# adaLN products in steps of 256 columns by half the features, the halves summed when evicted

## The chip, the cores and the metric

One NeuronCore of a Trainium2 chip runs the whole program. The metric is the device time of one execution in microseconds. The engines are named as in the profile: PE (matrix products; PEld are its weight loads), DVE, ACT and POOL (element-wise work), SP (issues DMAs). ACT and POOL issue DMAs too, each in its own queue of instructions.

## What is computed

Two layers of a hybrid backbone over 512 latent and 256 context tokens of 1024 features. Each layer starts with shift, scale and gate vectors from a conditioning vector, one for the latents (`c`) and one for the context (`c_ctx`):

```python
def layer_forward(x, xc, cos, sin, c, c_ctx, w_ada, b_ada, ...):
    shift, scale, gate = jnp.split(jax.nn.silu(c) @ w_ada + b_ada, 3, axis=-1)
    shift_c, scale_c, gate_c = jnp.split(jax.nn.silu(c_ctx) @ w_ada + b_ada, 3, axis=-1)
    h = rms_norm(x) * (1.0 + scale[:, None]) + shift[:, None]
...
    p = h @ w_in
...
    x = x + gate[:, None] * (jnp.concatenate([ya, yb, yc], axis=-1) @ w_out)
```

`w_ada` is 1024 x 3072 in float32 for each layer: 24 blocks of 128 columns, 8 each for shift, scale and gate. Between `p` and the last line stand three branches: a chunked MLP with gelu (`ya`), a bidirectional state-space scan, SSD (`yb`), and differential attention with four heads, rotary embedding and two score maps per head whose softmaxes are subtracted (`yc`). The second layer ends with a norm and updates only the latents.

## The kernel before

The program is written once for a layer and run for both. A scheduler places the instructions of all engines in one pass over a timeline of its own; the code gives it priorities (`HPada` and the like lift the DMAs of a block), `PACE` ties single projections to marks in the attention, so that the attention stays ahead of them, and buffers in rings (three of 512 KB, tag `raw`, for all weights that come from memory; two PSUM banks, tag `acc`, for projections and adaLN products). Each engine then runs its own list in order: an instruction that waits holds back all that follow it on that engine.

A layer runs in three stages. First the norm, the input projection of the SSD's blocks and the scan. Then the attention, from about 365 us in layer 0 and 1115 us in layer 1. Beside it PE works through the projections of the other branches: tiles `accz`, `accuv`, `accu`, `accga`, each a block of 128 columns in parts `hi` and `lo`. `scores` makes one score map (`sm`, L749 and L752), DVE its row maximum (`mx`, L754), ACT its exponentials (`Ea`, L756); `weights` transposes their difference (`ptw`, L777), `values` multiplies by v (`pO`, L790), normalises (`osq`, L791 and L798), transposes back (L799) and multiplies by the gate (`gg`, L801). `roped` loads a head's q or k block and its turned copy (`qrq`, `qrk`, `qsq`, `qsk`, L685 and L687) in SP's queue and rotates it on DVE (L689 to L691). Last the output projection: four groups of features (`kq` 4, 8, 0, 12 in layer 1), two halves of 512 columns, `oacc` L1025 to L1027. Its weights come as `wo` and are split into `wohi` on ACT and `wolo` on DVE (L145, L146). The mixed features are written to memory as `ydr` by `finish` (`yhi` and `ylo`, L434 in ACT's queue, L435 in POOL's) and are read back as `yl` (L1020, ACT's queue).

The shift, scale and gate of layer 0 that aren't needed at once are computed beside the attention by `ada_steps`: 24 steps in layer 0 (8 for its gate, 16 for layer 1's shift and scale) and 8 in layer 1 (its gate). A step is one block of 128 columns: SP loads it (`wa`, L194, 128 partitions x 8 x 128 float32), eight matmuls (L198) with 32 columns of weights each, `sc`, which are zero but for the two conditioning vectors, go to the four column groups of the array in turn, features 0 to 511 starting a sum in PSUM and features 512 to 1023 ending it, and ACT copies the bank to a quarter of `part` (L199). After four steps `ada_second` sums the four column groups with a matmul by `sel`.

Of the kernel before, what the change touches and what calls it, by code (L numbers as in the profile page):

```python
# [11 lines left out]
F32 = mybir.dt.float32  # L12
# [79 lines left out]
def tile_hybrid_trunk(ctx: ExitStack, tc: tile.TileContext, ins, out: bass.AP):  # L92
# [93 lines left out]
    def ada_steps(mp, todo):  # L186
        """todo: (layer, its index, first of four blocks); one step for each block"""
        pend = None
        for L, li, b0 in todo:
            part = mp.tile([P, 4, P], F32, tag="part", bufs=NPART, name=f"part{li}_{b0}")  # L190
            for i in range(4):
                with tc.high_priority(HPada):
                    wa = wpool.tile([P, KD, P], F32, tag="raw", bufs=NRAW, name=f"wa{li}_{b0}_{i}")
                    nc.sync.dma_start(wa, ins["w_ada"][li, :, P * (b0 + i) : P * (b0 + i) + P].rearrange("(k p) m -> p k m", p=P))  # L194
                pa = bank("acc", f"pa{li}_{b0}_{i}")
                for k in range(KD):
                    j = k % 4
                    pe.matmul(pa[32 * j : 32 * j + 32, :P], sc[:, k, :], wa[:, k, :], start=k < 4, stop=k >= 4)  # L198
                act.activation(part[:, i, :], pa[:, :P], AF.Copy)  # L199
                if pend:  # L200
                    ada_second(mp, *pend)
                    pend = None
                yield
            pend = L, li, b0, part
        ada_second(mp, *pend)
# [45 lines left out]
    def first_layer_in(L, sp, sx, ws, w_split):  # L251
        """norm and modulation of the inputs by feature blocks, the first projections beside it"""
# [6 lines left out]
        def ada_in(k):  # L259
            """shift and scale of feature block k"""  # L260
            with tc.high_priority((HPW0, HPW1, HPW)[min(k, 2)] if FL else HPW):
                wa = [sp.tile([P, KD, P], F32, tag="Fb", bufs=4, name=f"wa0_{k}_{i}") for i in range(2)]
                for i in range(2):
                    c0 = DM * i + P * k
                    nc.sync.dma_start(wa[i], ins["w_ada"][0, :, c0 : c0 + P].rearrange("(k p) m -> p k m", p=P))
            pa = bank("sc", f"pa0_{k}")
            for i in range(2):
                for q in range(KD):
                    j = q % 4
                    pe.matmul(pa[32 * j : 32 * j + 32, P * i : P * i + P], sc[:, q, :], wa[i][:, q, :], start=q < 4, stop=q >= 4)  # L270
            part = small.tile([P, 2, P], F32, tag="part0", name=f"part0_{k}")
            act.activation(part, pa[:, 0:256].rearrange("p (i m) -> p i m", i=2), AF.Copy)
            for i in range(2):
                pe.matmul(pa[:, 256 + 2 * i : 258 + 2 * i], part[:, i, :], sel, start=True, stop=True)
                dve.tensor_scalar(
                    L.mod[:, 8 * i + k, :], pa[:, 256 + 2 * i : 258 + 2 * i], L.b_ada[:, 8 * i + k : 8 * i + k + 1], float(i), ALU.add, ALU.add
                )
# [65 lines left out]
    for li in range(DEPTH):  # L343
# [67 lines left out]
        def silu_block(c0, name):  # L411
            """2 * silu of a projected block"""
# [16 lines left out]
        def finish(kt, y, t3=t3):  # L429
            """a finished block of the mixed features, in two parts"""  # L430
            hi = t3(f"yhi{li}_{kt}", dt=F32R)
            lo = t3(f"ylo{li}_{kt}", dt=F32R)
            split(hi[:, tl0:], lo[:, tl0:], y[:, tl0:])
            Q["yh"].dma_start(ydr[0, kt, :, tl0:], hi[:, tl0:].bitcast(F32))  # L434
            Q["yl"].dma_start(ydr[1, kt, :, tl0:], lo[:, tl0:].bitcast(F32))  # L435

        # ================= SSD =================
        with tc.tile_pool(name=f"ssd{li}", bufs=1, reuse_waits="tile") as sp, tc.tile_pool(name=f"ssx{li}", bufs=1, reuse_waits="tile") as sx, tc.tile_pool(name=f"ps_s{li}", bufs=3, space=PSUM, reuse_waits="tile") as ps2:
# [32 lines left out]
            def seg_proj(w, s, tag, name):  # L471
                """three passes of one block's product over one segment"""
# [82 lines left out]
            for g in range(2):  # L555
# [24 lines left out]
                def state(t, d, H_in):  # L580
                    """state after chunk t in direction d"""
# [76 lines left out]
            # projections that are kept for the attention  # L658
# [7 lines left out]
        # ================= attention; beside it the other branches' gates =================  # L666
        with ExitStack() as zstack, ExitStack() as mstack, ExitStack() as astack:
# [13 lines left out]
            def roped(idx, lonly, name):  # L681
                """a head's projected block, both parts of it, latents rotated"""
# [49 lines left out]
            def scores(H, h, t):  # L732
                """exponentials of one query tile's two (negated, scaled) score maps, their sums"""
# [27 lines left out]
            def weights(H, h, t, Es):  # L761
                """difference of the two maps, transposed"""
# [111 lines left out]
            def gelu2_block(c0, name):  # L874
                """2 * gelu of a projected block"""
# [98 lines left out]
        with tc.tile_pool(name=f"outa{li}", bufs=1, reuse_waits="tile") as oa, tc.tile_pool(name=f"outb{li}", bufs=1, reuse_waits="tile") as op, tc.tile_pool(name=f"ps_o{li}", bufs=NOA, space=PSUM, reuse_waits="tile") as ps2:  # L974
# [8 lines left out]
            # ================= output projection, gated residual =================  # L983
# [5 lines left out]
            for n in range(2):  # L989
# [20 lines left out]
                def product(t, qs):  # L1010
                    """part of one token tile's product"""
# [116 lines left out]
```

## Time and profile before

| | |
|---|---|
| median of three runs | 1448.0 us (1446.86 to 1449.85) |
| the profiled execution, its span | 1448.3 us |
| PE busy | 1337.9 us, 92% |
| DVE busy | 945.3 us, 65% |
| ACT busy | 656.1 us, 45% |
| POOL busy | 214.5 us, 15% |
| the chain that ended last | PE 53%, DMA 18%, issue 12%, DVE 9%, ACT 6% |
| `pa` matmul records beside the attention | 512, in 32 steps |

All durations below are from that one execution. A row of the timeline is the start, the duration, the engine with its line, the operation, output <- inputs, and how many like it follow one another; in brackets the idle time before it and what ended it. ACTq and SPq are those engines' DMA issues.

### The profile page before, as it was taken

Reading aid. Unit: us, or ns where it says so; the run is one execution under the profiler, and the core shown is the slowest. Engines: PE = TensorE matmul, PEld = TensorE weight load, DVE = VectorE, ACT = ScalarE, POOL = GpSimd, SP = SyncE. Lnnn points to the kernel's source line nnn. Section 1 sums busy time; section 2 is a strip of 40 time slices with the busy share of each in tenths; the row PEclk is TensorE's granted clock in tenths of the full one; section 3 lists DMA queues with packets and bytes.
Section 4 is the critical chain, followed back from the end, with each engine's and each line's share of the span. In section 5 each row is a group of like instructions: output and inputs, shape, how many; then the busy total and the mean of one; then the engine's idle time right before and its main releaser. Section 6 shows DMA issues by size and latency. Waiting matters only on the chain.

```text
span 1448.3 us, 21208 instructions
## 1 busy us (share of the span) xinstructions
PE 1337.9 (92%) x7944; PEld 1101.8 (76%) x7944; DVE 945.3 (65%) x1465; ACT 656.1 (45%) x1406; POOL 214.5 (15%) x418
## 2 busy tenths in 40 slices
PE   4999999999988999999999989999999689989987
PEld 3787888778867787788887768778778557778765
DVE  4497897587576657775232458887677477787432
ACT  3257634624455547554121235833623455575320
POOL 2002023113101113220000000202213001222000
PEclk8999999999999989999999999999999899989999
DMA  9424255745937447567878522625737954557885
GB/s 290 125 74 131 72 164 169 204 127 189 310 112 200 138 138 237 168 202 255 249 236 238 160 67 64 161 84 164 219 102 205 255 155 127 188 161 231 267 270 162
DMA packets 271782, 255.97 MB, mean 177 GB/s; under 512 B 14384, under 2 KB 223552, under 8 KB 271680
## 3 DMA queue, kind: packets, MB, share of 16 engines
q1 hardware_dynamic: 176624, 126.07, 31.1%
q0 software_dynamic: 18800, 66.68, 14.7%
q10 hardware_dynamic: 76256, 61.88, 13.9%
q8 instruction: 62, 1.02, 0.3%
q14 instruction: 40, 0.33, 0.1%
HBM read 199.12 MB, written 49.17 MB: 171 GB/s over the span
## 4 chain that ended last, share of the span: by engine, by line
PE 53%; DMA 18%; issue 12%; DVE 9%; ACT 6%; POOL 2%; SPq 1%; ACTq 0%; DVEq 0%; POOLq 0%
PE oacc L1027 4%; PE oacc L1026 4%; PE oacc L1025 4%; DMA Fb<-csd 3%; DMA yl<-ydr 3%; DMA qsq<-kq 2%; PE pS L585 2%; PE accc L387 2%; PE accc L391 2%; PE accc L392 2%; ACT Fb L608 2%; PE pO L790 2%; DMA qsk<-kq 2%; PE po L640 2%; PE acck L387 2%
## 5 line engine op out<-in xcount | busy, mean ns | idle before, releaser
L608 ACT ACTIVATE Fb<-Fb,dt_fp 128x128 f32<-128x128 f32 x320 | 98.6, 392 | 89.2 <-DVE Fb L605 89.2
L387 PE MATMUL accc<-h_hi,whic 128*128 128x512 f32 (+1 forms) x312 | 108.5, 348 | 5.5 <-ACT xp L451 3.8
L391 PE MATMUL accc<-h_lo,whic 128*128 128x512 f32 (+1 forms) x312 | 107.2, 344 | 0.0
L392 PE MATMUL accc<-h_hi,wloc 128*128 128x512 f32 (+1 forms) x312 | 106.8, 342 | 0.3 <-DVE wloc L146 0.3
L1025 PE MATMUL oacc<-wohi,yl 128*128 128x512 f32 x240 | 95.1, 396 | 5.0 <-DMA yl<-ydr 3.9
L1027 PE MATMUL oacc<-wohi,yl 128*128 128x512 f32 x240 | 95.4, 397 | 2.8 <-DMA yl<-ydr 2.8
L456 DVE SCALAR_TENSOR_TENSOR yv<-xp,hal,yv 128x772 f32<-128x772 f32 (+1 forms) x96 | 94.1, 993 | 5.7 <-ACT yv L454 4.5
L1026 PE MATMUL oacc<-wolo,yl 128*128 128x512 f32 x240 | 94.8, 395 | 1.0 <-DVE wolo L146 1.0
L756 ACT ACTIVATE Ea<-sm,mx 128x768 f32<-128x768 f32 (+1 forms) x80 | 65.2, 816 | 47.9 <-DVE mx L754 34.7
L605 DVE TENSOR_TENSOR Fb<-Fb,dt_cs 128x1024 f32<-128x1024 f32 x40 | 48.8, 1221 | 50.1 <-DMA Fb<-csd 50.0
L754 DVE TENSOR_REDUCE mx<-sm 128x1 f32<-128x768 f32 (+1 forms) x80 | 67.1, 843 | 13.6 <-PE sm L752 13.5
L387 PE MATMUL accz<-h_hi,whiz 128*128 128x512 f32 (+1 forms) x192 | 71.9, 375 | 0.8 <-DVE gtz L426 0.4
L391 PE MATMUL accz<-h_lo,whiz 128*128 128x512 f32 (+1 forms) x192 | 70.3, 366 | 0.0
L392 PE MATMUL accz<-h_hi,wloz 128*128 128x512 f32 (+1 forms) x192 | 70.1, 365 | 0.0
L387 PEld LDWEIGHTS accc<-h_hi,whic 128*128 128x128 f32 x312 | 59.4, 190 | 13.9 <-ACT xp L451 5.1
L749 PE MATMUL sm<-kh,qq 128*128 128x256 f32 (+1 forms) x144 | 52.5, 382 | 14.6 <-ACT Ea L756 12.9
L790 PE MATMUL pO<-v,wt 128*128 128x128 f32 x416 | 59.4, 295 | 6.5 <-DVE gg L801 4.8
L637 POOL DMA_DIRECT2D EF<-ecd x72 | 44.7, 627 | 139.3 <-DVE xT L642 128.3
L392 PEld LDWEIGHTS accc<-h_hi,wloc 128*128 128x128 f32 x312 | 59.5, 191 | 7.3 <-DVE wloc L146 0.5
L391 PEld LDWEIGHTS accc<-h_lo,whic 128*128 128x128 f32 x312 | 59.4, 190 | 6.8 <-issue 0.7
L790 PEld LDWEIGHTS pO<-v,wt 128*128 128x128 f32 x416 | 55.2, 207 | 11.6 <-DVE gg L801 5.5
L1043 DVE TENSOR_TENSOR go<-oacc,gate 128x512 f32<-128x512 f32 x20 | 13.7, 687 | 70.9 <-PE oacc L1027 70.9
(374 smaller groups left out, 3874.5 us busy)
## 6 DMA issues: line engine op xcount, KB each, us to landing
yl<-ydr ACTq DMA_DIRECT2D x120, 256.0 KB
wa<-in_w_ada SPq DMA_DIRECT2D x48, 512.0 KB
Fb<-csd POOLq DMA_DIRECT2D x40, 512.0 KB, 5.9
wo<-in_w_out SPq DMA_DIRECT2D x32, 512.0 KB
rawc<-in_w_in SPq DMA_DIRECT2D x22, 512.0 KB
EF<-ecd POOLq DMA_DIRECT2D x72, 128.0 KB, 3.1
rawz<-in_w_in SPq DMA_DIRECT2D x16, 512.0 KB
ydr<-yhi ACTq DMA_DIRECT2D x12, 384.0 KB
```

The lines of the kernel that those rows point to most:

```text
L387: m = pe.matmul(acc[:, :n], hi[:, k, :], h_hi[:, k, o : o + n], start=k == 0, stop=False)
L391: pe.matmul(acc[:, :n], hi[:, k, :], h_lo[:, k, o : o + n], start=False, stop=False)
L392: pe.matmul(acc[:, :n], lo[:, k, :], h_hi[:, k, o : o + n], start=False, stop=k == KD - 1)
L456: dve.scalar_tensor_tensor(yv[:, lo_:], xp[:, lo_ + tap : tap + W2], L.convh[:, j, tap : tap + 1], yv[:, lo_:], ALU.mult, ALU.add)
L608: act.activation(Fb[:, h, :], Fb[:, h, :], AF.Exp, bias=fp[:, o : o + 1])
L749: m = pe.matmul(c_, H.qs[i][:, tsl], H.kh[i][:, k0 : k0 + kn], start=True, stop=False)
L754: dve.tensor_reduce(mx[:, i : i + 1], smap[:, s0 : s0 + nk], AX.X, ALU.min)
L756: act.activation(Es[i], smap[:, s0 : s0 + nk], AF.Exp, bias=mx[:, i : i + 1], scale=-1.0, accum_out=z[:, i, t % 2 : t % 2 + 1])
L790: pe.matmul(o_, H.w[:, k, P * ql : P * ql + P], H.v[:, k, :], start=k == 0, stop=k == nkt - 1)
L1025: pe.matmul(accs[t], yh[0][:, k, :], whi, start=q == 0 and k == 0, stop=False)
L1026: pe.matmul(accs[t], yh[0][:, k, :], wlo, start=False, stop=False)
L1027: pe.matmul(accs[t], yh[1][:, k, :], whi, start=False, stop=q == 3 and k == 3)
```

## The change

Every step now takes 256 columns and half of the features. Four matmuls of 256 columns go to the four column groups, each starting and ending its sum. The first half's bank is copied by ACT to two quarters of `part`; the second half's bank is added to them by DVE. A step's load has the same 512 KB in rows of 1 KB instead of 512 bytes. The number of steps, the order of blocks, the buffers and the priorities are the same. The lines of the changed kernel behind this place are five higher. The rest of the diff takes comments and docstrings away.

```diff
-            for i in range(4):
-                with tc.high_priority(HPada):
-                    wa = wpool.tile([P, KD, P], F32, tag="raw", bufs=NRAW, name=f"wa{li}_{b0}_{i}")
-                    nc.sync.dma_start(wa, ins["w_ada"][li, :, P * (b0 + i) : P * (b0 + i) + P].rearrange("(k p) m -> p k m", p=P))
-                pa = bank("acc", f"pa{li}_{b0}_{i}")
-                for k in range(KD):
-                    j = k % 4
-                    pe.matmul(pa[32 * j : 32 * j + 32, :P], sc[:, k, :], wa[:, k, :], start=k < 4, stop=k >= 4)
-                act.activation(part[:, i, :], pa[:, :P], AF.Copy)
-                if pend:
-                    ada_second(mp, *pend)
-                    pend = None
-                yield
+            for c in range(2):
+                for half in range(2):
+                    r0, c0 = 4 * P * half, P * b0 + 256 * c
+                    with tc.high_priority(HPada):
+                        wa = wpool.tile([P, 4, 256], F32, tag="raw", bufs=NRAW, name=f"wa{li}_{b0}_{c}_{half}")
+                        nc.sync.dma_start(wa, ins["w_ada"][li, r0 : r0 + 4 * P, c0 : c0 + 256].rearrange("(k p) m -> p k m", p=P))
+                    pa = bank("acc", f"pa{li}_{b0}_{c}_{half}")
+                    for j in range(4):
+                        pe.matmul(pa[32 * j : 32 * j + 32, :256], sc[:, 4 * half + j, :], wa[:, j, :], start=True, stop=True)
+                    dst, pv = part[:, 2 * c : 2 * c + 2, :], pa[:, :256].rearrange("p (i m) -> p i m", m=P)
+                    if half == 0:
+                        act.activation(dst, pv, AF.Copy)
+                    else:
+                        dve.tensor_tensor(dst, dst, pv, ALU.add)
+                    if pend:
+                        ada_second(mp, *pend)
+                        pend = None
+                    yield
```

The scheduler runs anew, and from the first of these steps on the lists of all engines differ. Three places follow; in a name the first digit is the layer, the last number a running one.

DVE at the start of layer 0's attention, before: the rope products of head 1's q and k, then the first two reductions of score maps.

```order
L689 TENSOR_TENSOR qsk0_1_3571<-qsk0_1_3571,sin0_3405 128x512
L690 TENSOR_TENSOR qrq0_1_3588<-qrq0_1_3588,cos0_3404 128x512
L691 TENSOR_TENSOR qrk0_1_3569<-qrk0_1_3569,qsk0_1_3571 128x512
L754 TENSOR_REDUCE mx0_0_0_3458<-sm0_0_0_1_3459 128x1
L754 TENSOR_REDUCE mx0_0_0_3458<-sm0_0_0_0_3465 128x1
```

The same place after:

```order
L694 TENSOR_TENSOR qsk0_1_3571<-qsk0_1_3571,sin0_3405 128x512
L695 TENSOR_TENSOR qrq0_1_3588<-qrq0_1_3588,cos0_3404 128x512
L204 TENSOR_TENSOR part0_16_4689<-part0_16_4689,pa0_16_1_1_4946 128x256
L696 TENSOR_TENSOR qrk0_1_3569<-qrk0_1_3569,qsk0_1_3571 128x512
L759 TENSOR_REDUCE mx0_0_0_3458<-sm0_0_0_1_3459 128x1
L759 TENSOR_REDUCE mx0_0_0_3458<-sm0_0_0_0_3465 128x1
```

The addition of the second half has come between the rope products, ahead of the first reduction.

PE at the end of layer 1's attention, before: the last of the two transpositions of `pO1_3_2`, the last attention work, within the output product `oacc1_0`.

```order
L1025 MATMUL oacc1_0_3_12323<-wohi1_0_0_12256,yres1_0_12067 128x512
L799 MATMUL pO1_3_2_11071<-ident_75,osq1_3_2_11073 128x128
L1026 MATMUL oacc1_0_3_12323<-wolo1_0_0_12257,yres1_0_12067 128x512
L1027 MATMUL oacc1_0_3_12323<-wohi1_0_0_12256,yres1_1_12068 128x512
L1025 MATMUL oacc1_0_4_12368<-wohi1_0_2_12232,yl1_0_4_4_0_12369 128x512
```

After:

```order
L1032 MATMUL oacc1_0_5_12285<-wohi1_0_0_12128,yres1_1_11940 128x512
L804 MATMUL pO1_3_2_10975<-ident_75,osq1_3_2_10977 128x128 x2
L1030 MATMUL oacc1_0_2_12150<-wohi1_0_1_12134,yres1_0_11939 128x512
L1030 MATMUL oacc1_0_3_12195<-wohi1_0_1_12134,yres1_0_11939 128x512
L1030 MATMUL oacc1_0_4_12240<-wohi1_0_1_12134,yres1_0_11939 128x512
```

The last transposition stands 62 matmuls of the output product later, and the rows behind them are those that read `wohi1_0_1`.

ACT at the same place, before: from the last block's `yhi` to the loads of the last group of features.

```order
L145 ACTIVATE yhi1_15_11097<-gg1_3_10766 128x512
L434 DMA ydr1_7714<-yhi1_15_11097 128x512
L1020 DMA yl1_0_5_8_0_12430<-ydr1_7714 128x4x128
L1020 DMA yl1_0_5_8_1_12432<-ydr1_7714 128x4x128
L145 ACTIVATE wohi1_0_1_12262<-wo1_0_1_12260 128x1024
L145 ACTIVATE wohi1_0_6_12268<-wo1_0_6_12266 128x1024
L145 ACTIVATE wohi1_0_7_12274<-wo1_0_7_12272 128x1024
L1020 DMA yl1_0_2_12_0_12458<-ydr1_7714 128x4x128
```

After:

```order
L145 ACTIVATE yhi1_15_11001<-gg1_3_10670 128x512
L439 DMA ydr1_7618<-yhi1_15_11001 128x512
L1025 DMA yl1_0_2_12_0_12330<-ydr1_7618 128x4x128
L1025 DMA yl1_0_3_12_0_12353<-ydr1_7618 128x4x128
L1025 DMA yl1_0_4_12_0_12376<-ydr1_7618 128x4x128
L145 ACTIVATE wohi1_0_1_12134<-wo1_0_1_12132 128x1024
L145 ACTIVATE wohi1_0_6_12140<-wo1_0_6_12138 128x1024
L145 ACTIVATE wohi1_0_7_12146<-wo1_0_7_12144 128x1024
```

Three loads that read the `ydr` rows just written have moved ahead of the conversion `wohi1_0_1`. Further on, `yl1_0_5_12`, the last loads of the first half, stood behind the conversion of `wohi1_1_1` on ACT; now its two parts stand behind those of `wohi1_1_4` and `wohi1_1_5`, three and two conversions of second-half weights earlier.

## Rows read from the trace of the kernel before

**Rows 1.** The page, busy time of each engine, share of the span, instructions.

```profile
PE 1337.9 (92%) x7944; PEld 1101.8 (76%) x7944; DVE 945.3 (65%) x1465; ACT 656.1 (45%) x1406; POOL 214.5 (15%) x418
```

**Rows 2.** Windows: stretch, length, busy us of PE, PEld, DVE, ACT, POOL; clock; DMA share; GB/s.

```profile
365.00:400.00 35.00, 33.28 (x241) 27.90 (x238) 18.01 (x32) 15.62 (x31) 3.28 (x6) 1.00 1.03 312
1115.00:1357.00 242.00, 212.00 (x1179) 170.37 (x1178) 166.59 (x272) 128.26 (x269) 41.83 (x73) 0.94 0.66 194
1260.00:1280.00 20.00, 13.96 (x69) 10.29 (x67) 19.60 (x32) 15.71 (x35) 6.91 (x13) 0.80 0.74 226
```

**Rows 3.** The tile `pa`: count, ns min/median/max, first and last start, forms.

```profile
L198 PEld LDWEIGHTS pa<-wa,sc x512: 106/109/173, 373.1 to 1205.6; 128*32 128x32 f32 x171
L198 PE MATMUL pa<-wa,sc x512: 272/273/419, 373.1 to 1205.7; 128*32 128x128 f32 x171
...
L199 ACT ACTIVATE part<-pa x32: 259/277/300, 374.4 to 1206.9; 128x128 f32<-128x128 f32 x32
...
L272 ACT ACTIVATE part<-pa x8: 383/383/384, 22.1 to 59.9; 128x256 f32<-128x256 f32 x8
```

**Rows 4.** Timeline of PE: the first step of the products.

```profile
373.06 0.64 PE L198 MATMUL pa<-wa,sc 128*32 128x128 f32 x16
```

**Rows 5.** Timeline of DVE: an operation on two tiles of 128x256.

```profile
405.52 0.43 DVE L888 TENSOR_TENSOR gquv<-gquv,geuv 128x256 f32<-128x256 f32 x1
```

**Rows 6.** The page, DMA queues: packets, MB, share of 16 engines' span.

```profile
q1 hardware_dynamic: 176624, 126.07, 31.1%
q0 software_dynamic: 18800, 66.68, 14.7%
```

**Rows 7.** Timeline of SP's issues, start of layer 0's attention.

```profile
395.13 0.40 SPq L194 DMA_DIRECT2D wa<-in_w_ada  x1
402.03 0.53 SPq L687 DMA_DIRECT2D qsk<-kq  x1
```

**Rows 8.** Timeline of PE, DVE and ACT, end of layer 1's attention.

```profile
1356.73 0.27 PE L799 MATMUL pO<-ident,osq 128*128 128x128 f32 x1
...
1357.04 0.48 DVE L801 SCALAR_TENSOR_TENSOR gg<-gg,hal,pO 128x256 f32<-128x256 f32 x1 [7.77 <-PE pO L799]
...
1357.56 0.63 ACT L145 ACTIVATE yhi<-gg 128x512 fp32r<-128x512 f32 x1 [5.97 <-DVE gg L801]
1358.22 0.34 ACTq L434 DMA_DIRECT2D ydr<-yhi  x1
1360.02 0.98 ACTq L1020 DMA_DIRECT2D yl<-ydr  x2
1361.04 1.06 ACT L145 ACTIVATE wohi<-wo 128x1024 fp32r<-128x1024 f32 x1 [2.85 <-PE oacc L1027]
...
1362.74 0.37 ACTq L1020 DMA_DIRECT2D yl<-ydr  x1
```

**Rows 9.** The tile `ydr`, its stores from issue to landing.

```profile
DMA to landing us min/median/max: 2.3/3.8/7.8
```

**Rows 10.** Timeline of ACT and PE, the output product's change of halves in layer 1.

```profile
1375.54 1.06 ACT L145 ACTIVATE wohi<-wo 128x1024 fp32r<-128x1024 f32 x1 [1.60 <-DMA wo<-in_w_out]
...
1381.43 1.06 ACT L145 ACTIVATE wohi<-wo 128x1024 fp32r<-128x1024 f32 x1 [1.52 <-DMA wo<-in_w_out]
1381.51 0.94 ACTq L1020 DMA_DIRECT2D yl<-ydr  x2
...
1388.19 0.80 PE L1025 MATMUL oacc<-wohi,yl 128*128 128x512 f32 x1 [3.50 <-DMA yl<-ydr]
...
1390.42 0.80 PE L1027 MATMUL oacc<-wohi,yl 128*128 128x512 f32 x1 [1.00 <-DMA yl<-ydr]
```

**Rows 11.** The chain that ended last, same stretch: start, us, what.

```profile
1381.94 8.44 DMA yl<-ydr
...
1394.20 0.43 PE oacc L1026
...
1395.04 0.23 PE oacc L1025
```

## The prediction

> **What bounds the kernel now.** I read the page's busy times first. PE is busy 1337.9 of 1448.3 us [rows 1], so a change earns only where PE stands idle, or where its clock is down. The windows come next: they show where that is. In the first 35 us of layer 0's attention the DMA engines are full (share 1.03) while PE is busy 33.28 of 35; over layer 1's attention, 1115 to 1357 us, PE is busy 212.00 of 242, so 30 us are idle, and 20 us of it, 1260 to 1280, have PE 13.96 busy at clock 0.80 with DVE 19.60 busy [rows 2]. The tile view of `pa` gives the price of a step's parts [rows 3], the timeline one whole step [rows 4]. Last I followed the end of layer 1 in the timeline, since the order lists differ there most [rows 8 to 10].
>
> **The products.** A step before is eight fp32 matmuls, sixteen records, four at a time on the four column groups: 0.64 us from first start to last end [rows 4]. A step after is four matmuls, eight records, of twice the columns. If four still run at once, that is half as many rounds of twice the length, and nothing changes. If they ran one after another, eight records of two times 0.109 us (the median weight load, which paces them [rows 3]) make 1.74 us instead of 0.64: 32 x 1.10 = +35 us. Not needing to add up in PSUM could at best take the last round's tail away, 0.27 x 32 / 2 = -4 us. I take **0**, since the sixteen records in 0.64 us show the groups at work side by side and nothing in the change ties them together. All of it would lie on the path, PE being the bound.
>
> **The evictions.** ACT loses 32 x 0.277 = 8.9 us and gets 16 x 0.383 (a 128x256 eviction at the kernel's start) = 6.1 us [rows 3]. ACT is busy 45% [rows 1]: 2.7 us less there is worth nothing by itself. DVE gets 16 additions of 128x256; the nearest row is a 128x256 sum of two tiles, 0.43 us [rows 5], so 6.9 us on an engine that is 65% busy. An addition waits for its matmuls, and what is queued behind it on DVE waits too. At one place that is on the path: at the start of layer 0's attention the addition of `pa0_16_1_1` now stands between two rope products and ahead of `mx0_0_0`, the reduction for which the first exponentials wait. There it costs its 0.43 us, **+0.4**. Elsewhere the additions stand beside projections, and PE covers them; if all sixteen were on the path it would be +6.9.
>
> **The transfers.** Bytes and number of DMAs stay; packets go from 1024 of 512 bytes to 512 of 1 KB. Two queues give a price: q1 moved 126.07 MB in 176624 packets in 31.1% of 16 engines' span, which is 40.8 ns per packet of 714 bytes; q0 66.68 MB in 18800 packets in 14.7%, 181 ns per 3547 bytes [rows 6]. A line through both gives 30.8 ns for 512 bytes, 56.2 for 1 KB (an estimate): a step's transfer falls from 1.97 to 1.80 us of all sixteen engines, by 0.17. Only where the engines are full and an awaited load lies behind in SP's queue does it count. In the two attention starts seven `wa` issues stand ahead of an awaited `qsq` or `qsk` (one pair shown, `wa` at 395.13 and `qsk` at 402.03 [rows 7]): 7 x 0.17 = **-1.2**. The ends are 0 (the transfers hidden) and 32 x 0.17 = -5.4. The Trainium skill, "DMA: Bandwidth & Descriptors", section Specifications, puts the smallest transfer at line rate at 512 bytes; by that the packets before were as good as those after, the term would be 0 and the sum 1.2 us more. The two queues' prices don't settle it, since they hold other sizes too.
>
> **The order.** The scheduler places everything again, and from the first steps on the lists differ. Two places matter.
>
> *1260 to 1280 us.* Here PE has no projections, only score maps, and waits for DVE. After, a like run exists, earlier in the heads: six score maps again, with 30 DVE rows from the first reduction to the last instead of 35. With 19.60 us for 32 rows in the window [rows 2] five fewer are 3.0 us; half of the clock's loss, 20 x 0.20 x 13.96/20 / 2 = 1.4, goes with it: **-4.4**. Ends: 0 if DVE's rest is only moved, and 6.0 + 2.8 = -8.8 if all goes.
>
> *The end of layer 1's attention.* Before, the last transposition of `pO1_3_2` ends at 1357.0 and PE has 134 matmuls of the output product's first half left [rows 8], at 0.23 us each at full clock [rows 11]. After, both transpositions stand behind 120 of its 192 matmuls, and the next PE row needs `wohi1_0_1`. On ACT that conversion stood behind `yl1_0_5_8`; now it stands behind `yhi1_15`, its store to `ydr` and three loads of `yl` that read the store. So PE waits for a chain: from the transposition's end 0.04 to `gg`, 0.48, 0.04, `yhi` 0.63, 0.03, so the store's issue 1.2 us later [rows 8]; landing 2.3 us, the shortest of the `ydr` stores [rows 9] (the first load that reads this one went out at 1362.74, which bounds it at 4.5 [rows 8]); three loads at 0.49; the conversion 1.06 [rows 8]. 1.2 + 2.3 + 1.5 + 1.06 = **+6.0**, and 8.2 by the long landing. After waits of 3.50 and 1.00 us [rows 10] some twelve matmuls went 0.43 us apart instead of 0.23 [rows 11], at the lower of the clock's two levels: **+2.4** for a second such wait.
>
> Then the old wait. Before, PE waits 4.5 us for `yl1_0_5_12`, issued at 1381.51 behind the conversions of the second half's weights, which follow `wohi1_0_1` by 14.5 (`wohi1_1_5`) and 20.4 us (`wohi1_1_1`) [rows 8, 10]. After, the later of the two loads stands behind `wohi1_1_5`, so 15.6 us behind `wohi1_0_1`'s start; but from there PE has only 60 matmuls and the wait for a conversion left, 1.06 + 0.3 + 60 x 0.23 = 15.2 us. If the second load lands in 3.8 us, the median of the `ydr` stores [rows 9], PE waits 19.4 - 15.2 less some 0.5 of matmuls between, 3.7 us in sum; if it takes the 8.4 us that the one of 1381.94 took [rows 11], 8.2. The middle is 6.0, against 4.5: **+1.5** (-0.8 to +3.7).
>
> **The sum** on the profiled execution: 1448.3 + 0.4 - 1.2 - 4.4 + 6.0 + 2.4 + 1.5 = 1453.0; the median of the three runs is 0.3 below the span, so **1452.7**.
>
> **The rivals.** *Nothing to measure.* The wait for `wohi1_0_1` gives the DMAs time, and `yl1_0_5_12` lands before PE needs it: old wait and its slow matmuls vanish, 1452.7 - 1.5 - 4.5 - 2.4 = 1444.3 with the gain of 1260 to 1280, 1448.7 without it. It decides by whether `wohi1_1_5` is done 12 us after `wohi1_0_1` starts. For it: the loads stand two places earlier. Against it: the second half's weights can't load before the three conversions free their buffers. Middle 1446.5.
>
> *Faster.* The product rows that moved ahead of the last transposition, 62 of 0.23 us, are 14 us more work beside layer 1's attention, where 30 us are idle [rows 2]. If these fill 14 us there instead of my 4.4, the time is 1452.7 + 4.4 - 14 = 1443.1. It decides at 12 us filled. Against it: from 1280 to 1357 PE is nearly full before, and in the run of score maps DVE is the one that is short.
>
> *The column groups don't overlap at 256 columns:* 1452.7 + 35 = 1488. Only [rows 4] speaks on it, against.
>
> *The change doesn't do what it says* for the transfers, by the rule above: 1453.9, no other sign.
>
> **How the numbers follow.** Forecast (slower by 4 to 9 us) 0.47, nothing 0.26, faster 0.25, groups serial 0.02. About 0.2%, 2.9 us, is what a measurement can tell from no change. The forecast's case has a part within that bound and the rival of nothing a part beyond it on the fast side; I let them cancel. Slower 0.49, same 0.26, faster 0.25. The range: below, the faster rival with the whole DMA end, 1443.1 - 4.2 = 1438.9; above, the long landing (+2.2), the long old wait (+2.2) and no gain at 1260 (+4.4), 1461.5. The forecast's own range is 1448 to 1461.5.
>
> **What would show it.** Right: a step of `pa` about 0.64 us in eight records; PE waiting some 6 us straight behind the last two transpositions of `pO1_3_2`, released by ACT's `wohi`, with the clock down behind it; a wait for `yl` before the second half; `mx0_0_0` some 0.4 us later behind the addition. Wrong: no idle PE behind those transpositions (then the chain is hidden and the time is near 1445), a step over 1 us, or an attention stretch of layer 1 with under 20 us idle.

## The result, and the profile after

The changed kernel takes **1465.4 us** (median of 4 runs, 1458.9 to 1470.1) where the kernel before takes 1448.9 beside it: a ratio of 1.0114, with a 95% interval of 1.0081 to 1.0147, 16.5 us slower. The profiled execution took 1465.6 us. The forecast was 1452.7, with a range up to 1461.5.

PE's work is what the forecast said, and the price of a step too. The page's busy times and queues of the changed kernel, then its windows (columns as in [rows 2]), then the timeline of PE and the tile view of `part`:

```profile
PE 1335.3 (91%) x7688; PEld 1092.4 (75%) x7688; DVE 948.7 (65%) x1481; ACT 655.5 (45%) x1390; POOL 215.1 (15%) x418
...
q1 hardware_dynamic: 160240, 126.07, 30.6%
```
```profile
1115.00:1357.00 242.00, 208.24 (x1090) 166.36 (x1090) 166.09 (x274) 126.58 (x258) 42.66 (x72) 0.94 0.66 194
1260.00:1280.00 20.00, 15.53 (x84) 12.05 (x82) 17.47 (x32) 15.99 (x36) 8.12 (x13) 0.91 0.60 195
```
```profile
374.17 0.64 PE L199 MATMUL pa<-wa,sc 128*32 128x256 f32 x8
```
```profile
L202 ACT ACTIVATE part<-pa x16: 364/384/403, 375.5 to 1193.6; 128x256 f32<-128x256 f32 x16
...
L204 DVE TENSOR_TENSOR part<-part,pa x16: 398/414/423, 386.8 to 1204.3; 128x256 f32<-128x256 f32 x16
```

Against [rows 1] PE is busy 2.6 us less in a span 17.3 us longer, so the loss is idle time and clock. Against [rows 4] a step takes the same 0.64 us in half the records. Against [rows 2] the window 1260 to 1280 is better (15.53 busy for 13.96, clock 0.91 for 0.80), and the whole stretch from 1115 to 1357 is not (208.24 for 212.00).

Up to layer 1's first projection of `z`, some 40 us into its attention, the two profiled executions stand level (it starts at 1153.5 before and 1153.4 after). The last matmul of the output product ends at 1438.6 before and 1455.9 after. This is where the idle time stands in the changed kernel: the timeline of PE, rows that began late, with the idle time ahead and its releaser:

```profile
1339.04 0.47 PE L1030 MATMUL oacc<-wohi,yl 128*128 128x512 f32 x1 [2.83 <-DMA yl<-ydr]
...
1375.24 0.33 PE L804 MATMUL pO<-ident,osq 128*128 128x128 f32 x1 [0.46 <-ACT osq L803]
...
1381.58 0.79 PE L1030 MATMUL oacc<-wohi,yres 128*128 128x512 f32 x1 [6.00 <-ACT wohi L145]
...
1400.16 0.50 PE L1030 MATMUL oacc<-wohi,yl 128*128 128x512 f32 x1 [3.06 <-DMA yl<-ydr]
...
1406.94 0.77 PE L1030 MATMUL oacc<-wohi,yl 128*128 128x512 f32 x1 [3.44 <-DMA yl<-ydr]
...
1409.67 0.80 PE L1032 MATMUL oacc<-wohi,yl 128*128 128x512 f32 x1 [1.54 <-DMA yl<-ydr]
```

The wait of 6.00 is the one forecast. What the last three are shows in the count of `oacc` rows, of which a half has 192. The 3.06 stands behind row 180, like the two waits of [rows 10]: it is the old wait for `yl1_0_5_12`, 3.1 us where it had 4.5. The 3.44 and the 1.54 stand behind rows 192 and 194: they are for the first `yl` of the second half, 5.0 us that the kernel before does not have. The 2.83 at the first `yl` of the first half was not in the sum either. In the kernel before neither place has a wait; its timeline has the first row of either half without a bracket:

```profile
1340.27 0.39 PE L1025 MATMUL oacc<-wohi,yl 128*128 128x512 f32 x1
...
1394.85 0.41 PE L1025 MATMUL oacc<-wohi,yl 128*128 128x512 f32 x1
```

The last transposition ends at 1375.6 where it ended at 1357.0, and until then next to nothing is fetched. The windows of that stretch, first of the changed kernel, then of the kernel before; then, of the changed kernel, the DMA engines' share in 40 slices of 1357 to 1376 and the one queue that moved anything:

```profile
1357.00:1376.00 19.00, 18.11 (x94) 14.87 (x92) 1.03 (x3) 1.85 (x7) 0.70 (x1) 1.00 0.19 56
1376.00:1384.00 8.00, 2.42 (x6) 1.94 (x7) 3.23 (x5) 3.58 (x4) 1.12 (x2) 0.64 0.62 191
1384.00:1395.00 11.00, 11.00 (x48) 9.03 (x47) 3.51 (x3) 3.14 (x3) 0.00 (x0) 0.95 1.02 294
1395.00:1412.00 17.00, 8.91 (x30) 5.85 (x29) 10.34 (x12) 6.11 (x11) 0.00 (x0) 0.81 1.01 319
```
```profile
1357.00:1376.00 19.00, 19.00 (x86) 15.70 (x85) 8.35 (x8) 7.23 (x8) 1.12 (x2) 1.00 0.93 285
1376.00:1384.00 8.00, 8.00 (x37) 6.63 (x36) 5.22 (x6) 3.44 (x5) 0.00 (x0) 1.00 0.89 281
1384.00:1395.00 11.00, 6.50 (x17) 4.35 (x16) 2.33 (x4) 1.78 (x3) 0.00 (x0) 0.69 1.01 328
1395.00:1412.00 17.00, 17.00 (x77) 14.04 (x76) 6.52 (x9) 3.12 (x7) 0.76 (x2) 1.00 0.77 226
```
```profile
DMA  1699910000269950000000000000000000000000
...
q10 hardware_dynamic: 2146, 1.07, 19.4%
```

The DMA share is 0.19 while the attention's last block is at work, and 1.02 and 1.01 behind it. Before, it was 0.93 from 1357 to 1376. The reason is in the lists: `wo1_0_1`, `wo1_0_6` and `wo1_0_7` sit in the three `raw` buffers, and on ACT their conversions stand behind `yhi1_15`, which needs the attention's last transposition; so none of the eight loads of `wo1_1_*` can start. The waits of SP, which issues them, from 1339 to 1400:

```profile
SPq L1003 <- DVE wolo L146: 27.6, 7, 18.1
```

The longest, 18.1 us, ends when the first of the three is split. By the code the converted tiles also go into memory that the attention frees only with its last block; whether this alone would hold the conversions is not shown by any run. The chain that ended last (start, us, what) shows what follows, buffer by buffer:

```profile
1380.47 1.06 ACT wohi L145
...
1382.70 1.23 DVE wolo L146
...
1383.95 6.99 DMA wo<-in_w_out
...
1390.95 1.07 ACT wohi L145
...
1392.05 1.24 DVE wolo L146
...
1393.30 5.68 DMA wo<-in_w_out
...
1399.47 10.16 DMA yl<-ydr
...
1409.67 0.80 PE oacc L1032
```

Conversion, remainder, load, conversion, remainder, load, and then a load of `yl` that takes 10.16 us where the one of [rows 11] took 8.44.

The second place, to which e3 and e12 below led, is the start of layer 0's attention, on DVE. First the changed kernel, then the kernel before:

```profile
416.26 0.69 DVE L694 TENSOR_TENSOR qsq<-qsq,sin 128x512 f32<-128x512 f32 x1 [2.50 <-DMA qsq<-kq]
...
417.20 0.48 DVE L777 SCALAR_TENSOR_TENSOR Ea<-Ea,cz,Ea 128x256 f32<-128x256 f32 x1
```
```profile
412.31 0.48 DVE L772 SCALAR_TENSOR_TENSOR Ea<-Ea,cz,Ea 128x256 f32<-128x256 f32 x1
...
415.32 0.69 DVE L689 TENSOR_TENSOR qsq<-qsq,sin 128x512 f32<-128x512 f32 x1 [1.44 <-DMA qsq<-kq]
```

A rope product that waits for its load now stands ahead of the first weighted map `Ea`, and PE waits 4.2 us for that. The waits of PE, 405 to 425 (us in total, times, longest), the longest line after and before:

```profile
PE ptw L782 <- DVE Ea L777: 4.2, 1, 4.2
```
```profile
PE sm L749 <- ACT Ea L756: 2.9, 2, 2.2
```

### The profile page after: what moved, and what is told of

Same layout as the page of the kernel before. It is cut to its first block, busy times and chain, and to the rows that moved or that the text cites. A ratio compares the mean times of both kernels' runs of the same rounds, so it can differ in the third digit from the quotient of the medians.

```text
span 1465.6 us, 20682 instructions
## 1 busy us (share of the span) xinstructions
PE 1335.3 (91%) x7688; PEld 1092.4 (75%) x7688; DVE 948.7 (65%) x1481; ACT 655.5 (45%) x1390; POOL 215.1 (15%) x418
## 4 chain that ended last, share of the span: by engine, by line
PE 57%; DMA 19%; DVE 9%; issue 6%; ACT 6%; POOL 1%; SPq 1%; ACTq 0%; DVEq 0%; POOLq 0%
PE oacc L1032 4%; PE oacc L1030 4%; PE oacc L1031 4%; DMA Fb<-csd 3%; DMA qsq<-kq 2%; PE accc L392 2%; PE accc L396 2%; PE accc L397 2%; DMA yl<-ydr 2%; PE pO L795 2%; PE pS L590 2%; ACT Fb L613 2%; DMA wo<-in_w_out 2%; PE po L645 2%; PE accz L392 1%
## 5 line engine op out<-in xcount | busy, mean ns | idle before, releaser
L761 ACT ACTIVATE Ea<-sm,mx 128x768 f32<-128x768 f32 (+1 forms) x80 | 65.1, 815 | 52.2 <-DVE mx L759 30.9
L759 DVE TENSOR_REDUCE mx<-sm 128x1 f32<-128x768 f32 (+1 forms) x80 | 66.9, 843 | 14.5 <-PE sm L757 14.3
L146 DVE TENSOR_TENSOR wolo<-wo,wohi 128x1024 fp32r<-128x1024 f32 x32 | 38.8, 1223 | 39.2 <-ACT wohi L145 39.2
L1030 PEld LDWEIGHTS oacc<-wohi,yl 128*128 128x128 f32 x240 | 45.9, 191 | 22.4 <-DMA yl<-ydr 4.3
L145 ACT ACTIVATE wohi<-wo 128x1024 fp32r<-128x1024 f32 x32 | 33.5, 1056 | 55.8 <-DMA wo<-in_w_out 33.1
```

What stands on the lines that cost most here:

```text
L759: dve.tensor_reduce(mx[:, i : i + 1], smap[:, s0 : s0 + nk], AX.X, ALU.min)
L761: act.activation(Es[i], smap[:, s0 : s0 + nk], AF.Exp, bias=mx[:, i : i + 1], scale=-1.0, accum_out=z[:, i, t % 2 : t % 2 + 1])
L1030: pe.matmul(accs[t], yh[0][:, k, :], whi, start=q == 0 and k == 0, stop=False)
```

## The experiments

All ratios are to the kernel before on the same chip in the same job; its median was 1451.9 in the job of e1 to e4, 1451.5 for e5 to e8, 1452.9 for e9 to e11, 1450.0 for e12. So ratios are compared, at 14.5 us per 1%. *Theory "order"*: the loss is the scheduler's new order. *Rival "steps"*: it is what a step itself costs, wherever it stands.

**e1 and e2: the steps and the order apart.** Edges without a semaphore hold the instructions of each engine to a written order; nothing else is changed. e1 is the changed kernel in the order of before, e2 the kernel before in the order of the changed one.

```diff
+    by = {i.name: i for i in nc.cur_bb.bb.instructions}
+    for line in PLACED.values():
+        for a, b in zip(line, line[1:]):
+            tc.add_manual_dep(by[f"I-{b}"], f"I-{a}", NOSYNC, reason="placed")
```

> The changed kernel, its computation untouched, with every engine's list held in the order of the kernel before by ordering edges that add no wait (the four matmuls of a step stand where four of the eight stood, the first half's copy where it stood, the second half's addition on DVE where that step's copy stood in the whole program's order). Theory 'order' (the steps cost what they did, the loss comes from how the lists were laid anew): 1447 us, 1443 to 1451, the wait behind the last transpositions of layer 1 gone. Theory 'steps' (the loss lies in the 256-column matmuls, the 1 KB rows or the additions themselves): 1460 to 1470, as the changed kernel.

> The kernel before, its computation untouched, with every engine's list held in the order of the changed kernel (eight matmuls where four stood, a step's second copy on ACT at the place of the addition). Theory 'order': 1466 us, 1458 to 1471, with PE waiting some 6 us for wohi behind the last transpositions. Theory 'steps': 1449, as the kernel before.

Measured: e1 0.9974 (0.9951 to 0.9997), e2 1.0101 (1.0069 to 1.0133). The theory of the steps falls: the steps alone are 0.26% faster, 3.8 us, and the order alone costs 1.0%, 14.6 us. Together these two leave 0.75%; the changed kernel has 1.14%, and the intervals cover the difference.

**e3 and e12: where in the order.** e3 holds layer 1's attention and output to the order of before among themselves and leaves the rest as changed; e12 is the complement. The edit is that of e1, with two lists for an engine.

> The changed kernel; only the instructions of layer 1's attention and output stage are held in the order that they had before among themselves, all others in the changed kernel's own. If the whole loss lies in layer 1's attention and output: 1447 us, 1443 to 1451. If half of it comes from layer 0 and the scan: some 1457.

> The complement of e3_layer1_order_before: the changed kernel held to the order of the kernel before everywhere, except that layer 1's attention and output stand among themselves in the changed kernel's own order. Theory: the loss is the re-laid order of that stage alone, whatever happened ahead of it: from e1's 0.9974 the ratio rises by nearly the whole way to the changed kernel's 1.0114: 1.008 to 1.012 (1460 to 1466 where before stands at 1449). Rival: the order of the rest of the program costs its own part, as e3 suggests (1.0029, where e1 has 0.9974: 0.55% stayed although layer 1's attention and output stood as before): then only what e3 took away comes back, 1.0114 - 1.0029 = 0.85% over e1: ratio 1.004 to 1.0075 (1455 to 1460).

Measured: e3 1.0029 (1.0006 to 1.0052), e12 1.0066 (1.0044 to 1.0089). Layer 1's part of the order costs 0.85% by e3 against the changed kernel and 0.92% by e12 against e1, some 13 us. The order of the rest costs 0.55% (e3 against e1) or 0.48% (the changed kernel against e12), some 7 us: e12's rival was right, and that loss I had not looked for. Each of these differences is uncertain by 0.3 to 0.4%. The wait of PE for `Ea` on DVE shown above is there in the kernels with the changed order ahead of layer 1 (4.2 us in the changed kernel, 5.5 in e2, 4.5 in e3), and is 0.3 us or less in the others. The waits of PE, 405 to 425, in e1:

```profile
PE pv L904 <- DVE part L204: 1.9, 1, 1.9
PE sm L754 <- ACT Ea L761: 0.7, 1, 0.7
```

At layer 0's first projection of `z` (414.8 before) the changed kernel is 6.7 us late, e2 4.8, e3 5.2, e1 1.6 early, e12 0.6 early. Little of that is left later. Of the 14 profiled executions seven have the changed order ahead of layer 1 and seven the old one. They start layer 0's output product at 681.6 and 681.1 on average, and layer 1's first projection of `z` at 1153.6 and 1151.1, each group spread over 5 to 9 us. So the wait is seen, but not that it costs anything in the end; of the 7 us by the ratios the traces show 2.5 at layer 1's `z`, and where they are lost is open. The other part is plainer: from that `z` to the last matmul e1, e6 and e3 take 288.4, 288.8 and 291.9 us, the changed kernel, e2 and e12 302.5, 302.7 and 297.3.

**e4: the conversions ahead of the loads.** In the changed order, on ACT alone:

```diff
 ydr1<-yhi1_15
+wohi1_0_1, wohi1_0_6, wohi1_0_7
 yl1_0_2_12, yl1_0_3_12, yl1_0_4_12
-wohi1_0_1, wohi1_0_6, wohi1_0_7
```

> The changed kernel in its own order, but on ACT the three conversions wohi1_0_1, wohi1_0_6 and wohi1_0_7 stand ahead of the three loads yl1_0_2_12, yl1_0_3_12 and yl1_0_4_12 that wait for the store of yhi1_15. If that queue makes PE's 6.1 us wait, the landing (1.7 us) and the three issues (1.5 us) leave it: wait about 2.9 us, 1462 us or a little less. If the wait only moves on to the yl loads, which now go out 3 us later: 1465, with a longer wait for yl some 24 matmuls further on.

Measured: 1465.2 us, 1.008 (1.006 to 1.010). The waits of PE from 1330 on, e4:

```profile
PE oacc L1032 <- DMA yl<-ydr: 6.6, 3, 5.0
PE oacc L1030 <- DMA yl<-ydr: 2.8, 1, 2.8
PE oacc L1030 <- ACT wohi L145: 2.7, 1, 2.7
PE oacc L1030 <- DVE go L1048: 1.2, 1, 1.2
```

The wait behind the transpositions falls from 6.0 to 2.7, one of 5.0 for `yl` comes up 26 rows on, as the second reading of the expectation had it, and the 8.0 us behind rows 180 to 194 fall to 2.5. The waits trade places: from the transposition on they are 14.0 us in the changed kernel and 10.2 here. The ratio is 0.34% under the changed kernel's, in overlapping intervals; against 1448.9 it is 1460.5 us, near the time of the first reading.

**e6: the transfers alone.** The kernel before with the loads of the changed one, into the same tiles (the products then multiply other weights):

```diff
-nc.sync.dma_start(wa, ins["w_ada"][li, :, P * (b0 + i) : P * (b0 + i) + P].rearrange("(k p) m -> p k m", p=P))
+nc.sync.dma_start(wa.rearrange("p (k s) m -> p k (s m)", s=2), ins["w_ada"][li, 512 * (i % 2) : 512 * (i % 2) + 512, P * (b0 + i // 2 * 2) : P * (b0 + i // 2 * 2) + 256].rearrange("(k p) m -> p k m", p=P))
```

> The kernel before in its own order, with one line changed: each of the 4 loads of a group in the adaLN steps fetches 512 rows of w_ada by 256 columns (1 KB rows, as the changed kernel does) in place of 1024 rows by 128 columns (512 byte rows) into the same 512 KB tile. The products are left as they were, so they multiply the wrong weights, and the output is not the reference's; all work on the engines is the same. Theory A (what the steps alone gained in e1, ratio 0.9974, is the cheaper transfers, each of 32 steps taking about 0.3 us less of the 16 DMA engines): ratio 0.996 to 0.998, 1443 to 1446 where before stands at 1449. Theory B (the gain is TensorE's shorter steps beside the attention, or the addition moved from ScalarE to VectorE): ratio 0.999 to 1.001.

Measured: 0.9974 (0.9954 to 0.9994), as in e1, so the gain of the steps is, by these medians, that of their transfers, and shorter accumulation and the moved addition are worth nothing that shows. In e6 the page has

```profile
q1 hardware_dynamic: 160240, 126.07, 30.8%
```

against 31.1% in [rows 6]: 0.3% of 1448 us on all 16 engines, 4 us or some 0.14 per step, and about that much came off the time. The other profiled executions agree: the three with rows of 512 bytes (before, e2, e8) have 31.0 to 31.4%, 450 to 455 us of their spans, the ten with rows of 1 KB and all bytes 30.4 to 30.9%, 445 to 450 us. The averages are 5.9 us apart, 0.18 per step.

**e5 and e8: the old wait.** The two loads `yl1_0_5_12` one conversion further ahead on ACT, in the order of before, with the new steps (e5) and the old (e8):

```diff
+yl1_0_5_12_0, yl1_0_5_12_1
 wohi1_1_0
 wohi1_1_1
-yl1_0_5_12_0, yl1_0_5_12_1
```

> The changed kernel with every engine held to the order of the kernel before (as e1_after_order_before), but on ScalarE the two loads yl1_0_5_12 stand one conversion further ahead: before wohi1_1_0 instead of behind wohi1_1_1. Theory: the two waits of TensorE for yl behind 1384 (3.5 + 1.7 us in e1) come from the late issue of these loads (1382.8 in e1, landing some 6 us later); issued two conversions sooner (near 1376 to 1380) they end earlier, PE loses 3 to 5 us less there and keeps its full clock: 1443 to 1446 us, ratio 0.994 to 0.997 and 2 to 4 us under e1's 1449.0. Rival: the transfers are saturated in that stretch (DMA share 1.06 from 1384 to 1395 in e1), so that what lands sooner makes another block land later: no gain over e1, 1447.5 to 1450, ratio 0.997 to 1.000.

> The kernel before (its own steps and order) with the two loads yl1_0_5_12 issued ahead of ScalarE's conversion wohi1_1_0 instead of behind wohi1_1_1: the counterpart of e5_steps_yl_earlier without the new steps. Theory: the old wait (3.5 + 1.0 us of PE and the fall of the clock behind it) is the late issue: 1443 to 1446, ratio 0.996 to 0.998. Rival (transfers saturated, 1.01 from 1384 to 1395): 1448 to 1450, ratio 0.999 to 1.001.

Measured: e5 0.9978 (0.9955 to 1.0001), e8 0.9990 (0.9969 to 1.0012): nothing over their references, the rival's numbers both times. In e8 the wait has changed its name and its place: it now stands behind row 192, at the second half's start (timeline of PE, the one wait of a microsecond or more in the change of halves):

```profile
1394.12 0.47 PE L1025 MATMUL oacc<-wohi,yl 128*128 128x512 f32 x1 [3.23 <-ACT wohi L145]
```

The DMA engines are full there (share 1.01 in e8 from 1384 to 1395, as in the kernel before), and I read this as a load of weights coming later for the `yl` that came earlier, which is argued and not shown. In e5 the waits at the change of halves are 0.2, 2.0 and 0.7 us for `yl`, the last two in the second half. Moving this one load ahead in ACT's order gained nothing that shows.

**e7: half of the second half's weights.** The changed order; 256 KB instead of 512 for each `wo1_1_*`; the conversions read these columns twice, so columns 768 to 1023 of the output are made with the weights of 512 to 767.

```diff
-nc.sync.dma_start(raw, ins["w_out"][li, 2 * P * k2 : 2 * P * k2 + 2 * P, nsl].rearrange("(k p) m -> p k m", p=P))
+hw = li == 1 and n == 1
+nc.sync.dma_start(raw[:, :, :256] if hw else raw, ins["w_out"][li, 2 * P * k2 : 2 * P * k2 + 2 * P, slice(512, 768) if hw else nsl].rearrange("(k p) m -> p k m", p=P))
```

> The changed kernel in its own order, but of layer 1's second half of output weights only half is fetched (256 of 512 columns, 8 loads of 256 KB in place of 512 KB); the conversions read these columns twice, so that every engine does the same work, and columns 768 to 1023 of the output are computed from the wrong weights. Theory: the transfers are idle while the last block of layer 1's attention holds memory (DMA share 0.19 from 1357 to 1376) and saturated afterwards (1.02 and 1.01 from 1384 to 1412), and the waits of the second half's start (8.8 us from 1384 to 1412) and the slow clock behind them are that backlog: with 2 MB (some 7 us of transfers at 285 GB/s) less, 5 to 9 us go: 1456 to 1460, ratio 1.005 to 1.008. Rival: these waits are the order in which ScalarE issues the yl loads behind its conversions, whatever is queued at the DMA engines: 1463 to 1466, ratio 1.010 to 1.0115.

Measured: 1461.6 us, 1.0081 (1.0053 to 1.0108): 0.33% less than the changed kernel, the near end of what the theory gave, in overlapping intervals. The waits say it more plainly. Windows, and the rows of PE behind 1395 that began late:

```profile
1384.00:1395.00 11.00, 11.00 (x48) 9.05 (x47) 5.49 (x6) 4.13 (x4) 0.00 (x0) 0.96 0.84 237
1395.00:1412.00 17.00, 14.32 (x49) 10.65 (x48) 9.04 (x11) 6.80 (x12) 0.00 (x0) 0.80 0.98 300
```
```profile
1400.56 0.47 PE L1034 MATMUL oacc<-wohi,yl 128*128 128x512 f32 x1 [1.16 <-DMA yl<-ydr]
...
1402.78 0.80 PE L1036 MATMUL oacc<-wohi,yl 128*128 128x512 f32 x1 [1.52 <-DMA yl<-ydr]
```

2.7 us are left of 8.0, both rows at the second half's start, and PE is busy 14.32 of 17 for 8.91. So these waits go with the bytes that are still to be fetched. Whether they come from the queue at the DMA engines or from the chain of buffers shown above, whose loads are halved too, e7 does not tell apart.

**e9 to e11: fill the gap.** The raw tiles of `wo1_1_*` get two buffers of their own, in memory that held the attention's queries: in the changed order (e9), in that of before (e10), and in that of e4 (e11).

```diff
-raw = wpool.tile([P, 2, 512], F32, tag="raw", bufs=NRAW, name=f"wo{li}_{n}_{k2}")
+raw = (oa if li and n else wpool).tile([P, 2, 512], F32, tag="raw2" if li and n else "raw", bufs=2 if li and n else NRAW, name=f"wo{li}_{n}_{k2}")
```

> The changed kernel in its own order, with one line changed: the raw tiles of layer 1's second half of output weights (wo1_1_*) no longer share the three buffers raw with the first half; they have two buffers of their own, in memory that held the attention's queries and is free once the last score maps are done. No work changes. Theory: in the changed kernel the DMA engines stand idle from 1357 to 1376 (share 0.19) only because wo1_0_1, wo1_0_6 and wo1_0_7 hold the raw buffers until the attention's last block frees the memory of their converted tiles; with own buffers the first two blocks (1 MB, some 3.5 us of transfers at 285 GB/s) come in that gap, its DMA share rises to 0.35 or more, and the waits of the second half (8.0 us between 1395 and 1412) shrink by 3 to 5 us: 1460 to 1463, ratio 1.007 to 1.009. Rival: the transfers behind 1384 are not what these waits hang on: 1464 to 1467, ratio 1.010 to 1.0115, whatever the share in the gap.

> The changed kernel held to the order of the kernel before (as e1_after_order_before), with the two buffers of their own for wo1_1_* as in e9_after_own_staging. Theory: in this order the attention ends at 1357 and the DMA engines have no gap to fill (share 0.92 from 1357 to 1376, 1.06 from 1384 to 1395 in e1), so two more buffers bring little: the waits of 3.5 + 1.7 us stay within 2 us of that, ratio 0.996 to 0.998 as in e1 (0.9974). Rival: the three shared buffers held up the second half in this order as well: the waits go, and the time falls by 4 us or more under e1's, ratio 0.995 or less.

> The changed kernel's order with the three conversions wohi1_0_1, 6 and 7 ahead of the yl loads on ScalarE (as e4_wohi_first, 1465.2) and the two own buffers for wo1_1_* (as e9_after_own_staging). Theory: e4 took 3.4 us from the wait behind the last transpositions, and 5.1 us of a new wait for yl at 1387 took its place because the transfers were already behind; with the transfers started in the gap the new wait shrinks, so both gains show together: 1455 to 1461, ratio 1.004 to 1.0075. Rival: the new wait is the later issue of the yl loads by the three conversions (3.2 us of ScalarE), not the backlog: the same as e9 or slower than it, ratio 1.007 or more.

Measured: e9 1464.9 us, 1.0110 (1.0071 to 1.0148); e10 1456.2, 1.0024 (1.0000 to 1.0048); e11 1463.6, 1.0092 (1.0057 to 1.0127). For the time the rival of e9 was right, e10 came out slower than both readings of it, and e11 is no better than e4. The rows of PE in e9 that began late for `yl` up to 1400, and then the two longest waits at the change of halves:

```profile
1345.85 0.47 PE L1030 MATMUL oacc<-wohi,yl 128*128 128x512 f32 x1 [2.73 <-DMA yl<-ydr]
...
1349.88 0.50 PE L1032 MATMUL oacc<-wohi,yl 128*128 128x512 f32 x1 [1.99 <-DMA yl<-ydr]
...
1363.92 0.50 PE L1030 MATMUL oacc<-wohi,yl 128*128 128x512 f32 x1 [0.84 <-DMA yl<-ydr]
...
1365.31 0.50 PE L1032 MATMUL oacc<-wohi,yl 128*128 128x512 f32 x1 [0.23 <-DMA yl<-ydr]
...
1414.71 0.47 PE L1030 MATMUL oacc<-wohi,yl 128*128 128x512 f32 x1 [1.82 <-DVE wolo L146]
1415.96 0.70 PE L1032 MATMUL oacc<-wohi,yl 128*128 128x512 f32 x1 [0.55 <-DMA yl<-ydr]
```

The share from 1357 to 1376 rose to 0.76, and from the last transposition to the last matmul it took 74.0 us where the changed kernel took 80.3, as the theory wanted: of the 8.0 us at the change of halves 2.6 are left. But the wait of 1.99 was 0.69 in the changed kernel, and those of 0.84 and 0.23 are new: the weights fetched early stand beside the `yl` loads of the first half, and the way from the first `oacc` to the last transposition went from 36.5 to 41.0 us. Another 6.8 us were lost ahead of the first `oacc`; this execution is 7.6 us over e9's median. In e11 against e4 the last part is shorter too, 73.0 us for 78.4, the part before it 1.0 longer, and 6.2 us are lost ahead of the first `oacc`. Whether the moved tiles do that or it varies from run to run is open. So the gap has a large part in the waits at the change of halves, but filling it brought no time back, and no single edit of this stage undid what e3's whole order undoes.

## Why the prediction was wrong

The sign was right, the size was not: +4.7 us forecast, +16.5 measured. By the runs the 16.5 are -3.8 (steps), +7 (order ahead of layer 1's attention) and +13 (order from there on), each uncertain by some 5; the sum had -0.8, 0 and +5.5. The step that failed is "the order": two places were priced and all others taken as 0, and at the second place the waits were followed to the first half's last load and no further. The runs show in its place 5.0 us of waits at the second half's first `yl` and 2.8 at the first half's, both at 0 in the sum; a gain at the run of score maps that did not come in the profiled pair; and some 7 us in the order of the rest of the program, whose place stays open. Step by step:

- **Products, 0.** Right: 0.64 us in eight records, and e1 shows no cost of a step. The rival of serial groups is out.
- **Evictions, +0.4.** The price was right (0.414 us for 0.43). At the start of layer 0's attention I followed DVE's order to the first reduction `mx0_0_0` and stopped there. A few rows on stands `qsq0_1` ahead of `Ea0_0_0`, for which PE waits 4.2 us; the traces show little of that delay at layer 0's output product. "From the first steps on the lists differ" was in the text; two places were then priced and the rest taken as 0, for which e3 and e12 give some 7 us.
- **Transfers, -1.2.** Right sign, too small: -3.8 by e1 and e6, inside its ends (0 to -5.4) but near the far one. The price of a step fits, 0.17 us for 0.18 by the queue's shares (e6); I counted only seven loads ahead of an awaited one, and -3.8 would be some 22 steps at that price. The Trainium skill, "DMA: Bandwidth & Descriptors", section Specifications, has transfers at line rate from 512 bytes up, by which the gain would be 0; e6 disagrees, with the same bytes in 1 KB rows 0.26% faster.
- **The run of score maps, -4.4.** Too large. The window did improve (1.57 us more PE busy), but in the profiled pair the idle time went to other places of the same attention: PE waited 12.6 us for `Ea` from 1154 on, against 9.8 before. All waits from 1154 to the first `yl` are 19.1 us for 18.1, +1. Over all 14 executions they average 19.1 with the changed order of layer 1 and 21.3 with the old, each group spread over 6 us, so a gain of some 2 may be there. A window that gets better is not a stage that gets shorter; this was priced from a count of rows in one window.
- **The wait behind the last transpositions, +6.0.** Hit: 6.00 us, by the chain named, `yhi`, store, three loads, `wohi`. Its worth was less sure than its length (e4).
- **The first `yl`, 0.** Missed: 2.83 us. With 62 product rows moved ahead of the last transposition, the first half needs its loads earlier, and nothing in the sum asked whether they land by then.
- **The old wait, +1.5.** 3.1 us against 4.5, -1.4: a little under the lower end given (-0.8). I computed it from the order on ACT and the landing time of `yl`.
- **The second half's first `yl`, 0.** Missed: 5.0 us. Behind the old wait the sum looked no further. Ahead of it stand 19 us with almost no transfers and then all that was held back; with half the bytes 2.7 us of these waits and the old one together are left (e7), with the gap filled 2.6 (e9). The sentence against the first rival, that the second half's weights can't load before the three conversions free their buffers, was the mechanism, and I used it to choose between rivals and not in the sum.
- **The clock, +2.4.** Not measured by itself. From layer 1's first projection of `z` to the last matmul the profile has +17.4 (302.5 us for 285.1); 1, 2.8, 6.0, -1.4 and 5.0 of it are named, about 4 us remain, the clock among them (0.64, 0.95 and 0.81 in the windows from 1376, 1384 and 1395, where before it was 1.00, 0.69 and 1.00). Some 3 of the 17.4 may be the execution: e1 and e6, in the same order, took 288.4 and 288.8.

Of the rivals, "faster" had the right observation, 14 us of product moved beside the attention, and the wrong sign: the rows did not fill idle PE, they pushed the attention's end back. It comes 18.6 us later, 14 of them these rows' own time, and the conversions and loads that stand behind it come later with it.

The new steps in the order of before (e1: 0.9974) are the version that beats both kernels, by 0.26% over the kernel before, with an interval that ends at 0.9997.

## What to carry to other kernels

Where a scheduler places everything again, price a change in two parts, and measure it so: the edit held to the old order, and the old kernel in the new order; here they were -0.26% and +1.0%. When a stage's end moves, ask which conversions stand behind it, which buffers these hold, and which loads need the buffers; here PE was kept busy for 19 us in which the DMA engines had almost nothing to do. And follow an order past the first wait that it moves: one row that waits for a load, placed ahead of the row that the next engine needs, made PE wait ten times as long as the edit's own addition takes, and 5 us were waited for the loads behind those that were priced.

## What the runs showed of the hardware

Rows of 1 KB instead of 512 bytes, for the same 512 KB and the same number of DMAs, took 0.3% of the span off the 16 engines' time on queue q1 (31.1 to 30.8%) and 0.26% off the kernel (e6, between 0.06 and 0.46%). A 256 KB load of `yl` at the change of halves took 7.04 us in the chain of e6, 8.44 in [rows 11] and 10.16 in the changed kernel, whose DMA engines were full for longest (share 1.02 and 1.01 from 1384 to 1412; in the kernel before 1.01 to 1395 and then 0.77, in e6 1.02 and 0.82).
